# A hybrid encoder on one core: attention starts from half blocks kept in SBUF, and four smaller moves in the DeltaNet stage

## The chip, the cores and the metric

The kernel runs on 1 core of a Trainium2 chip. The metric is the device time of one execution in microseconds; three runs of the kernel before gave a median of 2773.81 us (2767.05 to 2774.55).

## The reference, cut to what matters

One encoder layer on two sequences, x_sample (2048 tokens) and x_prompt (1024 tokens), 1024 channels each, in float32. One projection feeds two branches, which are merged by gates.

```python
def _encoder_layer(x, ...):
    h = _rms_norm(x, norm_g)
    proj = jnp.einsum('btd,de->bte', h, w_in)
    qkv_a, z_a, qkv_b, z_b, beta_raw, alpha_raw, gate_a, gate_b = jnp.split(proj, split_points, axis=-1)
    ...
    o_a = _neighbourhood_attention(q_a, k_a, qkv_a[:, :, 2], rpb).reshape(B, T, NA_WIDTH) * jax.nn.silu(z_a)
    y_a = jnp.einsum('bte,ed->btd', o_a, w_branch_a)
    o_b = _deltanet_branch(qkv_b, z_b, beta_raw, alpha_raw, conv_w, a_log, dt_bias, dn_norm_g)
    y_b = jnp.einsum('bte,ed->btd', o_b, w_branch_b)
    merged = jax.nn.sigmoid(gate_a) * y_a + jax.nn.sigmoid(gate_b) * y_b
    return x + jnp.einsum('btd,de->bte', merged, w_out)
```

The DeltaNet branch convolves q, k and v along the tokens, and then runs one chunked delta-rule scan in each direction, for which it solves triangular systems (here: "inverses"). The attention branch has 8 heads of 64 and looks at a window of 8 rows by 16 columns on a grid 64 wide.

## The kernel before

The 3072 tokens are 6 blocks of 512, each in two half blocks of 256 columns; blocks 0 to 3 are the sample, 4 and 5 the prompt. The work comes in three stages.

**DeltaNet** (`deltanet()`). The normalised input is split into a high and a low float16 part, `hh` and `hl`, tiles of 128 x 8 x 256 in the pool `hp` with two buffers each; a copy of every half block is kept in DRAM (`hdr`). The projections' 36 tiles of 128 output channels (`Tile`, kinds r, z and g) go over the half blocks in five passes of twelve, n = 0 to 59: the first twelve come from the input, and the others are read back from `hdr` by four DMAs that `launch()` issues once half block n - 2 is used up. A tile on a half block is 24 products (`pp`) with the scaled weights `w`; ACT evacuates it (`evacuate`), kind g by a tanh into `thz` and a store to DRAM (`gtd`) for the last stage. The weights of later tiles come in by two generators `weights(0)` and `weights(1)`, half a tile each: a pass of maxima (`amax` on `wst`, tile `wm`), `factors()`, which reduces the maxima (`wma`), spreads them over the partitions by transposes on TensorE (`pm`) and makes scales of them, and then the split into float16 parts.

The order is a table of slots. `step_slot()` issues, on engines whose order is pinned to program order, what was put off to this slot, then a step of the scans (S), of the inverses (I), of weights (W) and rows (H), and of operands (O), with products from `products()` (`fill()`) poured between them up to a quarter, a half, three quarters and the whole of a slot's budget; `mids` and `ends_`, calls put there by `mid()` and `end()`, come at three quarters; then the finishing steps (F). A generator's `yield` ends its part of a slot, `yield 2` waits two slots. Where `fill()` has no product to give, it issues dummy transposes (`idle`) up to half the budget. `inverse()` reads the diagonal blocks of its matrices back from DRAM (`ed`) into `X` and `YT`, two slots later copies a part of `YT` transposed into `X` on ACT and on DVE, and works on from there; its sums run on DVE, and results go back through DRAM (`rd`, `RR`). `finish()` normalises a finished block: squares on ACT, a power on POOL (`af`), a scaling on ACT (`P<-P,af`), four transposes on TensorE (`ptf`), another scaling on ACT and a store (`obd`). At the stage's end `weights(1)` puts the first head pair's attention weights in DRAM (`wt`, `wt0` in the code), and `out_blocks()` prepares the output weights (`wod`).

**Attention**. For each of four head pairs, each block is projected by `proj_mm`, 4 tiles of tokens with 24 products each (`ppn`), with half blocks `H[b]` (`rh`, `rl`) as the stationary side and the pair's weights (`whi`, `wlo`) as the moving one. The blocks come in the order 4, 5, 0, 1, 2, 3. After the second block the first units (scores, exp, values) begin. `H` stays in SBUF through the stage: blocks 4 and 5 in the pool `h1`, the others in `hr`. In the fourth head pair, `branch_weights` puts the branch weights (`y`) in the places of blocks 4 and 5.

**Output**. The branch products are merged with the gates, and the last product is done.

At the boundary, deltanet's pools are closed, those of attention opened in the same SBUF, and 50 dummy transposes issued while the first weights and block 4 come in, pinned no longer: DMAs are ordered by a scheduler there.

Of the kernel before, what the change touches and what calls it, by code (L numbers as in the profile page):

```python
# [8 lines left out]
F32 = mybir.dt.float32  # L9
# [14 lines left out]
BLK = 512  # L24
# [21 lines left out]
def emit(nc, tc, x_prompt, x_sample, norm_g, w_in, attn_q_norm_g, attn_k_norm_g, attn_rpb, dn_conv_w, dn_a_log,  # L46
# [120 lines left out]
    def deltanet():  # L167
# [13 lines left out]
        ps_mm = opn("ps_mm", bufs=2, space=PSUM)  # L181
        hp = opn("hp", bufs=2, side="right")
        TR = (ps_tr, "tr", 4)


        sn = 0
        later, mids, ends_ = {}, [], []
        gens = {c: [] for c in "SOIFHW"}

# [26 lines left out]
        def fill(u):  # L216

            while T.cost < u:
                if not next(filler, 0):

                    t = ps_tr.tile([128, 4, 128], F32, name="idle", tag="tr") if T.cost < WARM * u else None
                    while T.cost < WARM * u:
                        T.transpose(t[:, 0, :], ident, ident)
                    return
# [39 lines left out]
        for n, t in enumerate(tiles):  # L264
            t.n = n
        wsc, wfc = (dcp.tile([128, NT + 5], F32, name=n) for n in ("wsc", "wfc"))
# [18 lines left out]
        def small():  # L285

            cwr = wk.tile([60, 128], F32, name="cwr", tag="gr", bufs=1)
# [12 lines left out]
            V.tensor_scalar_mul(nal, nal, -1.0)  # L300
# [136 lines left out]
        def staged(src, k):  # L437

            n = src.shape[0] // 256
            st = wk.tile([128, n, src.shape[1]], F32, name="wst", tag="xt", bufs=2)  # L440
            end(SY.dma_start, st, src[128 * n * k:128 * n * k + 128 * n].rearrange("(k p) c -> p k c", p=128))
            return st
# [41 lines left out]

        sb = wk.tile([128, 8, 16], F32, name="sb", tag="raw1")
        fba_ = []
# [8 lines left out]
        def bias_table():  # L495
# [6 lines left out]
            rp = wk.tile([120, 64], F32, name="rp", tag="gr", bufs=1)  # L502
            rp, ng = rp[:, 0:31], rp[:, 32:64]
# [13 lines left out]
            for ct in range(3):  # L517
                SY.dma_start(ud[16 * ct:16 * ct + 16].rearrange("i r k -> r i k"), ng[:, None, :].to_broadcast([120, 16, 32]))
            yield 3
            for ct, off in enumerate((0, -8, -16)):  # L520
# [9 lines left out]
        def weights(k):  # L530
# [9 lines left out]
            for p in range(1, 5):  # L540
# [3 lines left out]
                if k:  # L544
                    while maxed[0] < maxed[1]:
                        yield
                    yield from factors(ts[0].n, ts[-1].n + 1, ts)
                    facs[0] = p
                    yield
# [16 lines left out]
            while maxed[0] < maxed[1]:  # L566
                yield

            m1 = sm.tile([128, 2], F32, name="am1", bufs=1)
# [30 lines left out]
        def out_blocks(k):  # L600
# [4 lines left out]
            for i in range(k, 16, 2):  # L605
                p, q = divmod(i, 4)
                st = wk.tile([128, 4, 128], F32, name="wst", tag="raw1", bufs=2)
# [4 lines left out]
                hi, lo = (wk.tile([128, 7, 128], F16, name="wos", tag=t, bufs=2) for t in ("raw0", "raw2"))  # L612
                S.activation(hi[:, 0:3], st[:, 1:4], AF.Identity, scale=so4)
# [50 lines left out]
        def evacuate(t, n, pp):  # L664
            b, j = divmod(n, 2)
            f = wfc[:, t.n:t.n + 1]
            if t.kind == "r":
                if j == 0:
                    raws[t.h, b, t.i] = wk.tile([128, BLK + 4], F32, name=f"raw{t.i}")
# [7 lines left out]
            if t.kind == "g":  # L677
                SY.dma_start(gtd[n][t.i], th)
                return
# [78 lines left out]
        def tables(u):  # L758
# [48 lines left out]
            T.transpose(pr[:64, :], gc.rearrange("p a b -> p (a b)"), ident)  # L807
            gr = wk.tile([64, 128], F32, name="gr", tag="gr", bufs=1)
            V.tensor_copy(gr, pr[:64, :])
# [177 lines left out]
        def inverse(h, it):  # L987
# [4 lines left out]

            X = wk.tile([128, 1056], F32, name="X", bufs=1)
            U = wk.tile([128, 1024], F32, name="YT", bufs=1)
            W = wk.tile([128, 704], F32, name="Yo", bufs=1)
            Xr, Ur = (t[:, 0:1024].rearrange("p (r k) -> p r k", r=32) for t in (X, U))
# [4 lines left out]
            yield 2  # L1001
            S.activation(Xr[32:64], Ur[32:64].rearrange("p r k -> p k r"), AF.Copy)
            V.tensor_copy(Xr[96:128], Ur[96:128].rearrange("p r k -> p k r"))
            yield
# [58 lines left out]
            yield 1  # L1063
            RR = wk.tile([128, 2, 512], F32, name="RR", tag="X", bufs=1)
            Rc, Rt = (RR[:, q].rearrange("p (d c k) -> p d c k", d=2, c=8) for q in range(2))
# [73 lines left out]

            ZZ = wk.tile([128, 384], F32, name="ZZ", tag="YT", bufs=1)  # L1140
            Z = ZZ[:, 0:128].rearrange("p (c k) -> p c k", c=4)
# [77 lines left out]
        def finish(o):  # L1219
# [18 lines left out]
            for c in range(4):  # L1238
                T.transpose(pt[:, c, :], M[:, c, :], ident)
            ot = M.rearrange("p c t -> p (c t)")  # L1240
            S.activation(ot, pt.rearrange("p c t -> p (c t)"), AF.Identity, scale=dngz[:, o.h:o.h + 1])
# [11 lines left out]
        def launch():  # L1253
            l = todo["half"]
            if l and rel.get(l[0] - 2, sn) < sn:
                n = l.pop(0)
                t = half_tiles()
                for i in range(2):
                    for j in range(2):
                        f = SY.dma_start, t[i][:, 4 * j:4 * j + 4], hdr[n % 12 // 2][:, i, n % 2, 4 * j:4 * j + 4]  # L1260
                        if i + j:
                            at(i + j, *f)
                        else:
                            f[0](*f[1:])
                at(4, halves.__setitem__, n, t)
# [92 lines left out]
        while stk:  # L1358
            close(stk.pop())

    deltanet()

# [118 lines left out]
    def proj_mm(w, b, t):  # L1481

        hh, hl = H[b]
        ts = slice(128 * t, 128 * t + 128)
        pp = ps_mm.tile([128, 384], F32, name="ppn", tag="mm")
# [172 lines left out]
    def branch_weights(n):  # L1658

        for e in range(8):  # L1660
            if e % 2 == 0:
                y = h1.tile([128, 2, 2, 2, 4, 128], F16, name=f"y{e}", tag="h", bufs=4)
                for i in range(2):
                    for j in range(2):
                        wy[e + i, j] = y[:, i, j, 0], y[:, i, j, 1]
# [5 lines left out]
    for b in (4, 5, 0, 1, 2, 3):  # L1671
        H[b] = [(h1 if b > 3 else hr).tile([128, 8, BLK], F16, name=f"r{n}{b}", tag="h", bufs=4 if b > 3 else 8)
                for n in "hl"]
# [7 lines left out]

    t = ps_mm.tile([128, 256], F32, name="idle", tag="mm")
    for _ in range(50):
        T.transpose(t[:, 0:128], ident, ident)

    for k in (slice(0, 4), slice(4, 8)):
        for i, t in enumerate((w.hi, w.lo)):
            SY.dma_start(t[:, :, k], wt0[:, 3072 * i:3072 * i + 3072].rearrange("p (j k c) -> p j k c", j=3, k=8)[:, :, k])
            SY.dma_start(H[4][i][:, k, 0:HB], hdr[4][:, i, 0, k])
    for i in range(2):  # L1690
        SY.dma_start(H[4][i][:, :, HB:BLK], hdr[4][:, i, 1])
    w.p = [abp[:, 4 + j:5 + j] for j in range(3)]
    pair_scales(w, V)
    load_H(5)

# [248 lines left out]
    for hp_ in range(4):  # L1944
        if hp_:
            w = nxt
        if hp_ < 3:
            nxt = pair(hp_ + 1)
            next_pair(nxt)
        for b, ats in ((4, ()), (5, (5, 4)), (0, ()), (1, (0,)), (2, (1,)), (3, (2, 3))):  # L1950
            if hp_ == 3 and b == 0:
# [7 lines left out]
            if hp_ == 0 and b in (4, 5, 0, 1):  # L1959
                with tc.issue_after(anchors[b].ins):  # L1960
                    load_H((2, 3, None, None, 0, 1)[b])
            for a in ats:
# [67 lines left out]
    while stk:  # L2030
        close(stk.pop())
    close(p_cp)
    close(p_dr)
# [22 lines left out]
```

## Time and profile before

| | |
|---|---|
| runs, median | 2773.81 us |
| profiled execution | 2774.7 us, span 2772.9 us |
| TensorE busy | 2693.2 us, 97% |
| mean granted TensorE clock | 0.993 |
| dummy transposes | 274, 36.4 us |
| last product of DeltaNet ends about | 1654.4 us |
| first product of attention | 1668.0 us |

In the rows of a timeline stand the start, the length, the engine, the instruction with what it writes and reads, how often in a row, and in brackets how long the engine had been idle and what ended that. An instruction's length overlaps with its neighbours' on TensorE, so counts of them are best costed by the length of a row with many. Nearly every instruction has line 61, a helper that pins the order, so groups go by tiles.

### The profile page before, as it was taken

The page shows a single profiled execution, that of the slowest core. Times are in us where ns is not written, and L with a number is a line of the kernel's source. Part 1 is how long each engine was busy: PE and PEld are TensorE (multiplying, and loading weights), DVE is VectorE, ACT ScalarE, POOL GpSimd, SP SyncE. Part 2 cuts the span into 40 slices and gives each one's busy share as a digit, 9 for nine tenths or more (in the row PEclk, how much of TensorE's full clock was granted, in tenths as well). Part 3 has the DMA queues.
Part 4 walks back from the last instruction along what each step waited for, and adds up shares of the span by engine and source line. Part 5 has one row for each costly group of instructions (what it writes and reads, how often), then busy time and mean ns, then how long its engine had stood idle before and what let it go on. Part 6 is the DMA issues. An engine that isn't in the chain of part 4 may idle for free.

```text
span 2772.9 us, 65318 instructions
## 1 busy us (share of the span) xinstructions
PE 2693.2 (97%) x25080; PEld 2160.1 (78%) x25080; DVE 1763.7 (64%) x4099; ACT 1392.1 (50%) x3861; POOL 962.9 (35%) x1737
## 2 busy tenths in 40 slices
PE   7999999999999999999999999999999999999999
PEld 6888888988889888999888896666666666776675
DVE  6767866576775766747666423666666677556654
ACT  4455564555545655455554534666666764211211
POOL 2233231231222322222322305445444444554453
PEclk9999999999999999999999999999999999999999
DMA  7433442354533444323446648433332565444341
GB/s 244 156 118 92 126 128 85 106 150 112 131 101 104 131 135 127 89 89 108 123 118 179 187 126 222 120 112 89 102 94 86 151 205 200 167 168 158 115 146 69
DMA packets 503974, 365.02 MB, mean 132 GB/s; under 512 B 146035, under 2 KB 452847, under 8 KB 502767
## 3 DMA queue, kind: packets, MB, share of 16 engines
q1 hardware_dynamic: 503663, 360.85, 43.7%
q8 instruction: 198, 3.24, 0.5%
q14 instruction: 113, 0.93, 0.1%
HBM read 262.53 MB, written 98.20 MB: 130 GB/s over the span
## 4 chain that ended last, share of the span: by engine, by line
PE 73%; DVE 11%; DMA 5%; ACT 4%; SPq 3%; issue 2%; POOL 1%; DVEq 0%; POOLq 0%; ACTq 0%
PE pp L61 31%; PE ppn L61 10%; PE pk L61 6%; SPq L61 3%; DVE YT L61 2%; PE pT L61 2%; PE pS L61 2%; PE lv L61 2%; PE pon L61 1%; DVE P L61 1%; DVE Yo L61 1%; PE gq L61 1%; ACT P L61 1%; PE ptk L61 1%; PE idle L61 1%
## 5 line engine op out<-in xcount | busy, mean ns | idle before, releaser
L61 PE MATMUL pp<-hh,w 128*128 128x256 f16 x6912 | 1197.1, 274 | 13.7 <-DVE thz L61 8.4
L61 PEld LDWEIGHTS <-w 128*128 128x128 f16 x10368 | 1013.8, 99 | 146.0 <-issue 13.3
L61 PE MATMUL pp<-hl,w 128*128 128x256 f16 x3456 | 948.4, 274 | 6.1 <-DMA hl<-hdr 3.8
L61 PE MATMUL ppn<-whi,rh 128*128 128x384 f16 x768 | 250.4, 326 | 1.6 <-ACT qs L61 1.6
L61 PEld LDWEIGHTS <-y 128*128 128x128 f16 x2304 | 224.7, 98 | 34.7 <-issue 6.6
L61 PE MATMUL ppn<-whi,rl 128*128 128x384 f16 x768 | 251.3, 327 | 0.0
L61 PE MATMUL ppn<-wlo,rh 128*128 128x384 f16 x768 | 250.4, 326 | 0.0
L61 PEld LDWEIGHTS <-rh 128*128 128x128 f16 x1536 | 144.6, 98 | 71.7 <-issue 1.8
L61 POOL TENSOR_TENSOR th<-th 128x128 f32<-128x128 f32 (+1 forms) x240 | 148.2, 635 | 145.7 <-DVE th L61 132.5
L61 PEld LDWEIGHTS <-mm 128*128 128x128 f16 x1008 | 98.6, 98 | 115.2
L61 ACT ACTIVATE thz<-pp,wfc 128x256 f32<-128x256 f32 x288 | 124.0, 472 | 122.5 <-PE pp L61 92.7
L61 ACT ACTIVATE mm<-th 128x256 f16<-128x256 f32 x144 | 58.9, 445 | 227.9 <-POOL th L61 227.9
L61 DVE TENSOR_TENSOR pl<-pT,ph 128x384 f16<-128x384 f32 (+1 forms) x192 | 110.8, 599 | 82.1 <-ACT ph L61 80.8
L61 POOL TENSOR_TENSOR rqk<-rqk,mhalf 128x4 f32<-128x4 f32 x48 | 51.9, 1081 | 293.7 <-DVE rqk L61 287.3
L61 DVE CUSTOM_DVE_ANT_0 Sb<-pS,bt 128x384 f32<-128x384 f32 (+1 forms) x192 | 108.8, 598 | 67.0 <-DMA vd<-vt 23.5
L61 ACT ACTIVATE vn<-pk,nbeg 128x128 f32<-128x128 f32 x176 | 65.1, 370 | 160.6 <-PE pk L61 160.2
L61 ACT ACTIVATE Sb<-Sb,nm,pq 128x384 f32<-128x384 f32 (+1 forms) x192 | 140.0, 733 | 1.2 <-DVE nm L61 1.1
L61 PEld LDWEIGHTS <-rl 128*128 128x128 f16 x768 | 74.9, 98 | 61.2 <-issue 30.1
L61 ACT ACTIVATE raw<-pp,wfc 128x256 f32<-128x256 f32 x144 | 63.7, 472 | 116.7 <-PE pp L61 113.7
L61 ACT ACTIVATE Os<-pon,rsn 128x64 f32<-128x64 f32 x192 | 49.9, 312 | 142.8 <-PE pon L61 142.7
L61 DVE SCALAR_TENSOR_TENSOR P<-raw,cw,P 128x512 f32<-128x512 f32 x144 | 116.1, 806 | 0.6
L61 DVE SCALAR_TENSOR_TENSOR S<-S,egl,pk 128x128 f32<-128x128 f32 x160 | 54.8, 343 | 91.2 <-PE pk L61 67.1
(621 smaller groups left out, 5653.4 us busy)
## 6 DMA issues: line engine op xcount, KB each, us to landing
wst<-in_w_in SPq DMA_DIRECT2D x124, 256.0 KB
gtd<-thz SPq DMA_DIRECT2D x192, 128.0 KB
hh<-hdr SPq DMA_DIRECT2D x96, 256.0 KB
hl<-hdr SPq DMA_DIRECT2D x96, 256.0 KB
th<-gtd SPq DMA_DIRECT2D x24, 1024.0 KB
vw<-vd SPq DMA_DIRECT2D x320, 64.0 KB
IT<-gd SPq DMA_DIRECT2D x48, 256.0 KB
bt<-ud SPq DMA_DIRECT2D x256, 48.0 KB
```

The costliest lines, as they stand in the source:

```text
L61: i = f(*a, **k)
```

## The change

Seven edits:

- The pool `hp` is opened ahead of `deltanet()` and stays open; the last two half blocks (n = 58 and 59, block 5) are kept as `kept`. Attention does block 5 first, from them, and block 4 second; block 4 alone is loaded at once, and block 5's copies in `h1` are gone. Half of the branch weights go to the two places of `hp`.
- The 50 dummies are gone, and `fill()` issues none once all 24 blocks have had their last transposes (`finished`).
- Tiles whose last use is early (X, YT, Yo, raw, staged weights and some small ones) go to a pool `we` on the right side of SBUF, where attention later has its first weights.
- The stores of the last four gate tiles on the last three half blocks (twelve DMAs) are issued from ACT's queue.
- The first two copies of each inverse are put to the slot's end (`end`).
- The generators of weights wait one slot more between the last maximum and `factors()`, and between the last maximum and the last scales.
- The three stores of the bias table's blanks come two slots apart.

```diff
+        we = opn("we", bufs=2, side="right")
...
             while T.cost < u:
                 if not next(filler, 0):
+                    if finished[0] == 4 * NB:
+                        return
...
-            t.n = n
+            t.n, t.last = n, n > len(tiles) - 5
...
-            yield 3
+                yield 2
+            yield
...
                     while maxed[0] < maxed[1]:
                         yield
+                    yield
                     yield from factors(ts[0].n, ts[-1].n + 1, ts)
...
-                SY.dma_start(gtd[n][t.i], th)
+                (S if t.last and n > 8 else SY).dma_start(gtd[n][t.i], th)
...
-            X = wk.tile([128, 1056], F32, name="X", bufs=1)
+            X = we.tile([128, 1056], F32, name="X", bufs=1)
...
             yield 2
-            S.activation(Xr[32:64], Ur[32:64].rearrange("p r k -> p k r"), AF.Copy)
-            V.tensor_copy(Xr[96:128], Ur[96:128].rearrange("p r k -> p k r"))
+            end(S.activation, Xr[32:64], Ur[32:64].rearrange("p r k -> p k r"), AF.Copy)
+            end(V.tensor_copy, Xr[96:128], Ur[96:128].rearrange("p r k -> p k r"))
             yield
...
                 T.transpose(pt[:, c, :], M[:, c, :], ident)
+            finished[0] += 1
...
+                if n >= 58:
+                    kept[n - 58] = t
...
+    p_hp, hp = pool("hp", bufs=2, side="right")
+    kept = {}
     deltanet()
...
-        hh, hl = H[b]
-        ts = slice(128 * t, 128 * t + 128)
+        hh, hl = H[b] if b < 5 else kept[t // 2]
+        ts = slice(128 * (t if b < 5 else t % 2), 128 * (t if b < 5 else t % 2) + 128)
...
-                y = h1.tile([128, 2, 2, 2, 4, 128], F16, name=f"y{e}", tag="h", bufs=4)
+                if e < 4:
+                    y = h1.tile([128, 2, 2, 2, 4, 128], F16, name=f"y{e}", tag="h", bufs=2)
+                    y = y[:, 0], y[:, 1]
+                else:
+                    y = [hp.tile([128, 2, 2, 4, 128], F16, name=f"y{n}{e}", tag=n) for n in ("hh", "hl")]
...
-    t = ps_mm.tile([128, 256], F32, name="idle", tag="mm")
-    for _ in range(50):
-        T.transpose(t[:, 0:128], ident, ident)
-
     for k in (slice(0, 4), slice(4, 8)):
         for i, t in enumerate((w.hi, w.lo)):
             SY.dma_start(t[:, :, k], wt0[:, 3072 * i:3072 * i + 3072].rearrange("p (j k c) -> p j k c", j=3, k=8)[:, :, k])
-            SY.dma_start(H[4][i][:, k, 0:HB], hdr[4][:, i, 0, k])
-    for i in range(2):
-        SY.dma_start(H[4][i][:, :, HB:BLK], hdr[4][:, i, 1])
...
-    load_H(5)
+    load_H(4)
...
-        for b, ats in ((4, ()), (5, (5, 4)), (0, ()), (1, (0,)), (2, (1,)), (3, (2, 3))):
+        for b, ats in ((5, ()), (4, (5, 4)), (0, ()), (1, (0,)), (2, (1,)), (3, (2, 3))):
```

On TensorE at the boundary, this stands in the program before (`pp` is DeltaNet's product, `ptf` the last two blocks' transposes, `ppn` attention's first products; LDWEIGHTS is the load of the stationary side):

```order
22910 L61 MATMUL pp<-hl,w 128x256
22911 L61 LDWEIGHTS w
22912 L61 MATMUL pp<-hh,w 128x256
22913 L61 MATMUL idle<-ident 128x128 x30
22914 L61 MATMUL ptf<-ident,P 128x128 x8
22915 L61 MATMUL idle<-ident 128x128 x84
22916 L61 LDWEIGHTS rh_23722
22917 L61 MATMUL ppn<-whi,rh_23722 128x384
```

In the change the only dummies near the end stand ahead of the last half block's products, and then the first projection follows, on the kept half block:

```order
22716 L61 MATMUL pp<-hl,w 128x256
22717 L61 LDWEIGHTS w
22718 L61 MATMUL pp<-hh,w 128x256
22719 L61 MATMUL idle<-ident 128x128 x17
22720 L61 LDWEIGHTS w
22721 L61 MATMUL pp<-hh,w 128x256
```

```order
22910 L61 MATMUL pp<-hl,w 128x256
22911 L61 LDWEIGHTS w
22912 L61 MATMUL pp<-hh,w 128x256
22913 L61 LDWEIGHTS hh
22914 L61 MATMUL ppn<-whi,hh 128x384
```

114 dummies have become 17, the eight `ptf` now stand at 22840, ahead of the last 36 products, and the stationary side of `ppn` is `hh` instead of `rh`.

On DVE at the fifth inverse (`X<-YT` is its first copy, `thz<-thz,pp` the evacuation that frees a bank for TensorE, `P` and `Vt` with `raw` are steps of the convolution, `w` is a weight's low part), before:

```order
801 L61 SCALAR_TENSOR_TENSOR t<-pk,egc,Vt 128x128
802 L61 COPY X<-YT 32x1024
803 L61 SCALAR_TENSOR_TENSOR w<-wst,wsc,w 128x512 x2
804 L61 SCALAR_TENSOR_TENSOR P<-raw_8328,cw,P 128x512
805 L61 SCALAR_TENSOR_TENSOR Vt<-raw_8652,cw,Vt 128x512
806 L61 SCALAR_TENSOR_TENSOR thz<-thz,pp 128x256
```

and in the change:

```order
801 L61 SCALAR_TENSOR_TENSOR t<-pk,egc,Vt 128x128
802 L61 SCALAR_TENSOR_TENSOR P<-raw_8333,cw,P 128x512
803 L61 SCALAR_TENSOR_TENSOR Vt<-raw_8657,cw,Vt 128x512
804 L61 COPY X<-YT 32x1024
805 L61 SCALAR_TENSOR_TENSOR thz<-thz,pp 128x256
806 L61 MEMSET X 128x32
807 L61 SCALAR_TENSOR_TENSOR w<-wst,wsc,w 128x512 x2
```

Two steps of the convolution have moved ahead of the copy, the weight's low part behind it, and `thz` stands right behind the copy. At the first inverse the step `P<-raw_1836,P`, which `ptk` on TensorE reads, has moved from behind the copy to ahead of it in the same way.

On SP at the boundary (`gtd<-thz` are the gate stores, `obd<-P` finished blocks, `rh` and `rl` block 4), before:

```order
682 L61 DMA gtd_100<-thz 128x256 x4
683 L61 DMA whi<-wt_102 128x3x512
684 L61 DMA rh_23722<-hdr_69 128x4x256
685 L61 DMA obd_76<-P 128x512
686 L61 DMA obd_75<-P 128x512
687 L61 DMA wlo<-wt_102 128x3x512
688 L61 DMA rl_23723<-hdr_69 128x4x256
```

and in the change, where the weights are issued:

```order
662 L61 DMA wt_102<-w 128x1024 x2
663 L61 DMA obd_72<-P 128x512
664 L61 DMA whi<-wt_102 128x3x512
665 L61 DMA wlo<-wt_102 128x3x512
666 L61 DMA whi<-wt_102 128x3x512
667 L61 DMA gtd_96<-thz 128x256 x2
668 L61 DMA wlo<-wt_102 128x3x512
669 L61 DMA hh<-hdr_69 128x1024
```

The weights' loads have moved from behind the last gate stores to right behind the stores of `wt`, ahead of the loads of half block 57 (`hh<-hdr_69`) and of the last two; block 4's copies stand at 684, behind `obd_75`, `otn` and three loads of `bt`.

More of the change, by code (lines that the diff above doesn't have):

```diff
@@ L181, in deltanet @@
         ps_mm = opn("ps_mm", bufs=2, space=PSUM)
-        hp = opn("hp", bufs=2, side="right")
+        we = opn("we", bufs=2, side="right")
         TR = (ps_tr, "tr", 4)
@@ L187, in deltanet @@
         later, mids, ends_ = {}, [], []
+        finished = [0]
         gens = {c: [] for c in "SOIFHW"}
@@ L285, in small @@
         def small():
-            cwr = wk.tile([60, 128], F32, name="cwr", tag="gr", bufs=1)
+            cwr = we.tile([60, 128], F32, name="cwr", tag="gr", bufs=1)
             SY.dma_start(cwr, dn_conv_w[0].rearrange("t (g p) -> (t g) p", p=128))
@@ L439, in staged @@
             n = src.shape[0] // 256
-            st = wk.tile([128, n, src.shape[1]], F32, name="wst", tag="xt", bufs=2)
+            st = we.tile([128, n, src.shape[1]], F32, name="wst", tag="xt", bufs=2)
             end(SY.dma_start, st, src[128 * n * k:128 * n * k + 128 * n].rearrange("(k p) c -> p k c", p=128))
@@ L483, in first_weights @@
                 yield
-        sb = wk.tile([128, 8, 16], F32, name="sb", tag="raw1")
+        sb = we.tile([128, 8, 16], F32, name="sb", tag="raw1")
         fba_ = []
@@ L501, in bias_table @@
                 SY.dma_start(gk2[64 * j:64 * j + 64], attn_k_norm_g[0].rearrange("(p o) -> p o", o=1))
-            rp = wk.tile([120, 64], F32, name="rp", tag="gr", bufs=1)
+            rp = we.tile([120, 64], F32, name="rp", tag="gr", bufs=1)
             rp, ng = rp[:, 0:31], rp[:, 32:64]
@@ L567, in weights @@
                 yield
+            yield
             m1 = sm.tile([128, 2], F32, name="am1", bufs=1)
@@ L606, in out_blocks @@
                 p, q = divmod(i, 4)
-                st = wk.tile([128, 4, 128], F32, name="wst", tag="raw1", bufs=2)
+                st = we.tile([128, 4, 128], F32, name="wst", tag="raw1", bufs=2)
                 for j, (a, b) in enumerate(((0, 1), (0, 0), (1, 0), (1, 1))):
@@ L611, in out_blocks @@
                 yield 2
-                hi, lo = (wk.tile([128, 7, 128], F16, name="wos", tag=t, bufs=2) for t in ("raw0", "raw2"))
+                hi, lo = (we.tile([128, 7, 128], F16, name="wos", tag=t, bufs=2) for t in ("raw0", "raw2"))
                 S.activation(hi[:, 0:3], st[:, 1:4], AF.Identity, scale=so4)
@@ L668, in evacuate @@
                 if j == 0:
-                    raws[t.h, b, t.i] = wk.tile([128, BLK + 4], F32, name=f"raw{t.i}")
+                    raws[t.h, b, t.i] = we.tile([128, BLK + 4], F32, name=f"raw{t.i}")
                 S.activation(raws[t.h, b, t.i][:, 2 + HB * j:2 + HB * j + HB], pp, AF.Identity, scale=f)
@@ L807, in tables @@
             T.transpose(pr[:64, :], gc.rearrange("p a b -> p (a b)"), ident)
-            gr = wk.tile([64, 128], F32, name="gr", tag="gr", bufs=1)
+            gr = we.tile([64, 128], F32, name="gr", tag="gr", bufs=1)
             V.tensor_copy(gr, pr[:64, :])
@@ L991, in inverse @@
             rd = dr.tile([2, 8, 4, 32, 32], F32, name=f"rd{h}{it}")
-            X = wk.tile([128, 1056], F32, name="X", bufs=1)
-            U = wk.tile([128, 1024], F32, name="YT", bufs=1)
-            W = wk.tile([128, 704], F32, name="Yo", bufs=1)
+            X = we.tile([128, 1056], F32, name="X", bufs=1)
+            U = we.tile([128, 1024], F32, name="YT", bufs=1)
+            W = we.tile([128, 704], F32, name="Yo", bufs=1)
             Xr, Ur = (t[:, 0:1024].rearrange("p (r k) -> p r k", r=32) for t in (X, U))
@@ L1063, in inverse @@
             yield 1
-            RR = wk.tile([128, 2, 512], F32, name="RR", tag="X", bufs=1)
+            RR = we.tile([128, 2, 512], F32, name="RR", tag="X", bufs=1)
             Rc, Rt = (RR[:, q].rearrange("p (d c k) -> p d c k", d=2, c=8) for q in range(2))
@@ L1138, in level4 @@
                     V.tensor_copy(u.E[u.A:u.A + 64, :, u.B:u.B + 64], lv[u.A:u.A + 64])
-            ZZ = wk.tile([128, 384], F32, name="ZZ", tag="YT", bufs=1)
+            ZZ = we.tile([128, 384], F32, name="ZZ", tag="YT", bufs=1)
             Z = ZZ[:, 0:128].rearrange("p (c k) -> p c k", c=4)
@@ L1661, in branch_weights @@
             if e % 2 == 0:
-                y = h1.tile([128, 2, 2, 2, 4, 128], F16, name=f"y{e}", tag="h", bufs=4)
+                if e < 4:
[3 more added lines that the diff above has]
+                    y = [hp.tile([128, 2, 2, 4, 128], F16, name=f"y{n}{e}", tag=n) for n in ("hh", "hl")]
                 for i in range(2):
                     for j in range(2):
-                        wy[e + i, j] = y[:, i, j, 0], y[:, i, j, 1]
+                        wy[e + i, j] = y[0][:, i, j], y[1][:, i, j]
             for j in range(2):
@@ L1670, in emit @@
     H = [None] * NB
-    for b in (4, 5, 0, 1, 2, 3):
-        H[b] = [(h1 if b > 3 else hr).tile([128, 8, BLK], F16, name=f"r{n}{b}", tag="h", bufs=4 if b > 3 else 8)
+    for b in (4, 0, 1, 2, 3):
+        H[b] = [(h1 if b > 3 else hr).tile([128, 8, BLK], F16, name=f"r{n}{b}", tag="h", bufs=2 if b > 3 else 8)
                 for n in "hl"]
@@ L1960, in emit @@
                 with tc.issue_after(anchors[b].ins):
-                    load_H((2, 3, None, None, 0, 1)[b])
+                    load_H((2, 3, None, None, 1, 0)[b])
             for a in ats:
@@ L2031, in emit @@
         close(stk.pop())
+    close(p_hp)
     close(p_cp)
```

## The prediction

> **What bounds the kernel now.** I read the page first, then PE's waits, then PE's timeline around each wait, then the other engines there, and last the granted clock by windows.
>
> ```profile
> span 2772.9 us, 65318 instructions
> PE 2693.2 (97%) x25080; PEld 2160.1 (78%) x25080; DVE 1763.7 (64%) x4099; ACT 1392.1 (50%) x3861; POOL 962.9 (35%) x1737
> 1600.00:1620.00 20.00, 20.00 (x184) 18.61 (x182) 5.78 (x20) 7.05 (x21) 0.00 (x0) 1.00 0.37 119
> ```
>
> The span is TensorE's: it is busy for 2693.2 of 2772.9 us, and in a stretch near the end of DeltaNet for 20.00 of 20.00 (third row: window, its length, then each engine's busy time, TensorE first, the granted clock, the DMA share and GB/s). The change takes no product away, so it can save three things: TensorE's idle time (79.7 us in all), dummy transposes that count as busy, and time at a lower clock. The waits of TensorE (engine, tile, what it waited for, us in total, times, longest) show where the idle time lies:
>
> ```profile
> PE pp L61 <- DVE thz L61: 8.6, 5, 3.1
> PE ptk L61 <- DVE P L61: 5.0, 4, 3.2
> PE pm L61 <- DVE wma L61: 3.7, 3, 2.6
> PE pp L61 <- DMA hl<-hdr: 3.8, 2, 3.3
> ```
>
> Each of these totals is mostly one or two single waits, so each can be looked up. The timeline of the boundary, where DeltaNet ends and attention begins (start, length, instruction, count):
>
> ```profile
> 1640.76 0.61 PE L61 MATMUL pk<-vn,IT 128*128 128x128 f32 x4
> 1654.42 3.44 PE L61 MATMUL idle<-ident 128*128 128x128 f32 x30
> 1657.69 1.04 PE L61 MATMUL ptf<-ident,P 128*128 128x128 f32 x8
> 1658.57 9.60 PE L61 MATMUL idle<-ident 128*128 128x128 f32 x84
> 1668.00 0.33 PE L61 MATMUL ppn<-whi,rh 128*128 128x384 f16 x1
> 1655.40 2.44 ACT L61 ACTIVATE P<-P,af 128x128 f32<-128x128 f32 x8
> 1657.61 0.37 SPq L61 DMA_DIRECT2D whi<-wt  x1
> 1663.57 1.00 SPq L61 DMA_DIRECT2D rl<-hdr  x1
> ```
>
> TensorE does 114 dummy transposes between the last projection of DeltaNet and the first of attention, because the weights (whi) and block 4 (rh, rl) are issued only from 1657.61 on. The page calls this busy.
>
> **Part by part: the boundary.** The 114 dummies cost 3.44 + 9.60 = 13.04 us, 0.114 us each. The order of the change has 17 there, 1.95 us, and the first projection follows at once on the last DeltaNet product: -11.1 us. Elsewhere it has 163 dummies for 160: +0.3. What covers the rest:
>
> ```profile
> 1643.99 10.59 PE pp L61 x97
> 1668.17 14.14 PE ppn L61 x86
> 1674.41 2.00 SPq L61 DMA_DIRECT2D rl<-hdr  x1
> 1670.43 0.10 PEld L61 LDWEIGHTS <-rl 128*128 128x128 f16 x1 [0.38 <-DMA rl<-hdr]
> ```
>
> A DeltaNet product takes 10.59/97 = 0.109 us, an attention one 14.14/86 = 0.164. The last transposes (ptf) need a chain through DVE, ACT, POOL and ACT again that took 16.3 us here (pk's end at 1641.4 to 1657.69); in the change 156 products and the 17 dummies stand in between, 19.0 us, so ptf should not wait. Weights: issued two half blocks early. Block 4 is now the second block, wanted 4 x 24 x 0.164 = 15.7 us after the first projection. Its copy stands on SP behind two stores of P that follow ptf, a load of otn and three of bt. Estimate: ptf ends 36 x 0.109 = 3.9 us before the first projection, the stores land at most 5.9 us after their issue (rl took 1670.43 - 1664.57 = 5.9 from issue to use, with much in flight), and I give ACT's copies and SP's issues 3 us, so block 4 is issued from 5.0 us on; at 2.0 us a DMA (1674.41) its first half is issued by 9.0 and lands by 14.9 of 15.7. The nearest other case, block 5 in this trace, was issued to 1676.4 and wanted at 1668.2 + 15.7 = 1683.9 without a wait. I take zero, and 0 to 5 us as the bounds. Swapping blocks 4 and 5, and putting the later branch weights where the kept halves were, adds no instruction: zero, covered by the three blocks between the last read of the halves and their overwriting.
>
> **The inverses' first copies.** They are ACT and DVE instructions that wait for a DMA, and everything queued behind them waits too:
>
> ```profile
> L61 ACT ACTIVATE X<-YT 32x1024 f32<-32x1024 f32 x12 | 23.9, 1996 | 13.9 <-DMA YT<-ed 13.7
> 205.84 1.06 DVE L61 COPY X<-YT 32x1024 f32<-32x1024 f32 x1 [3.80 <-DMA YT<-ed]
> 209.92 0.63 PE L61 MATMUL ptk<-ident,P 128*128 128x128 f32 x4 [3.16 <-DVE P L61]
> 664.27 1.07 DVE L61 COPY X<-YT 32x1024 f32<-32x1024 f32 x1 [4.54 <-DMA YT<-ed]
> 668.03 0.41 DVE L61 SCALAR_TENSOR_TENSOR thz<-thz,pp 128x256 f32<-128x256 f32 x1
> 668.49 0.37 PE L61 MATMUL pp<-hh,w 128*128 128x256 f16 x1 [3.14 <-DVE thz L61]
> 1023.09 1.06 DVE L61 COPY X<-YT 32x1024 f32<-32x1024 f32 x1 [3.81 <-DMA YT<-ed]
> 1027.31 0.27 PE L61 MATMUL pp<-hh,w 128*128 128x256 f16 x1 [2.40 <-DVE thz L61]
> ```
>
> Three of twelve inverses reach TensorE: 3.16, 3.14 and 2.40 us. In the change the product for ptk (P) stands ahead of the copy, so the first goes. In the other two, thz stands right behind the copy instead of five instructions behind it: at 668 it would end at 664.27 + 1.07 + 0.41 = 665.8 instead of 668.4, which leaves some 0.5 us of the wait (TensorE had arrived at 668.49 - 3.14 = 665.35); at 1027 it goes. That is 3.16 + 2.7 + 2.4 = 8.3 us. The copy itself is 2.0 us on ACT and delays the same slot's end; X's next user, a memset a slot later, has the time.
>
> **The extra yield before the scale factors.**
>
> ```profile
> 1331.30 0.69 DVE L61 TENSOR_REDUCE wm<-wst 128x1 f32<-128x512 f32 x1 [2.99 <-DMA wst<-in_w_in]
> 1332.87 0.16 DVE L61 TENSOR_REDUCE wma<-wm 128x4 f32<-128x8 f32 x1
> 1333.17 0.76 PE L61 MATMUL pm<-ident,wma 128*128 128x128 f32 x4 [2.65 <-DVE wma L61]
> ```
>
> TensorE stood 2.65 us at transposes whose input DVE was late with. A slot later the input is long there: -2.65. The weights come a slot later for it; the dummies, which count the starved slots, hardly change (+3), so I cost that at zero.
>
> **The clock.** After such waits the granted clock (third number from the end) is down:
>
> ```profile
> 668.00:672.00 4.00, 3.51 (x20) 2.87 (x20) 2.46 (x9) 3.46 (x8) 2.53 (x3) 0.58 0.62 197
> 672.00:676.00 4.00, 4.00 (x39) 3.63 (x38) 3.79 (x11) 0.69 (x2) 0.96 (x1) 1.00 0.00 0
> 200.00:220.00 20.00, 16.84 (x213) 14.80 (x211) 13.15 (x26) 8.56 (x23) 8.47 (x14) 0.91 0.54 186
> 660.00:680.00 20.00, 16.86 (x142) 14.82 (x141) 13.82 (x33) 11.73 (x31) 6.76 (x10) 0.91 0.36 101
> 1320.00:1340.00 20.00, 17.35 (x258) 13.87 (x257) 13.60 (x28) 10.78 (x34) 9.29 (x18) 0.91 0.66 194
> 1020.00:1040.00 20.00, 17.60 (x161) 15.85 (x160) 15.46 (x35) 13.00 (x37) 6.24 (x10) 1.00 0.46 123
> ```
>
> 20 x 0.09 = 1.8 us are lost behind each of three of the waits, none behind the one at 1027: another -5.4 if these waits go. The Trainium skill's page "TensorE: Matmul & The Clock Gate", Part 1, has the clock fall to half rate after an idle window of about 3.4 us, and speaks for dummies wherever a wait could be that long. By it none of these waits (3.16, 3.14, 2.65 us) would have cost clock, this term would be nothing and the time 2757.9. The rows show the half rate (0.58 over 4 us) but already behind 2.65 us, so they decide: -5.4.
>
> **Stores and the rest.** Twelve gate stores (gtd) move to ACT's queue, where each takes issue time:
>
> ```profile
> 1631.04 0.79 SPq L61 DMA_DIRECT2D gtd<-thz  x2
> L61 ACT ACTIVATE thz<-pp,wfc 128x256 f32<-128x256 f32 x288 | 124.0, 472 | 122.5 <-PE pp L61 92.7 <-issue 28.3 <-ACT Yo L61 0.5
> ```
>
> 0.4 us each, and ACT has per pair of evacuations 48 x 0.109 = 5.2 us for 2 x 0.47 + 2 x 0.4 + at most 2.44 (P<-P,af) = 4.2: hidden. The bias table's pauses move SP work that no TensorE wait follows: zero. The weights' four loads go ahead of a half block's on SP; bound 0 to 5 us, taken as zero, since TensorE lacked nothing in that stretch (1600 to 1620, above).
>
> **Sum.** -11.1 + 0.3 - 8.3 - 2.65 - 5.4 = -27.1 us. Other order also makes other waits; I allow one new wait like the largest that stays:
>
> ```profile
> 617.28 0.37 PE L61 MATMUL pp<-hl,w 128*128 128x256 f16 x1 [3.30 <-DMA hl<-hdr]
> 617.00:621.00 4.00, 3.72 (x39) 2.59 (x42) 3.96 (x8) 0.00 (x0) 1.51 (x4) 0.61 1.00 309
> ```
>
> 3.30 + 4 x 0.39 = 4.9 us. So -22.2. The profiled execution took 2774.7 us with its span of 2772.9, 0.9 us above the median of the runs (2773.81); 2774.7 - 22.2 = **2752.5 us**, span near 2750.7. A measurement of this kernel can tell about 0.3%, 8.3 us, from no change.
>
> **Rivals.**
> - Waits only move: the DMAs land no sooner, and other work then stands behind the copies. For it: the copies' DMA waits stay on the queues. Against it: the named products are ahead of them. Only the boundary counts: 2774.7 - 10.8 = 2764.
> - Block 4 or the early weights come late: 5 us and a clock loss of 1.7 at one place, 2752.5 + 6.7 = 2759. For it: 14.9 of 15.7 us above.
> - Slower: ACT, in order, must wait at each store until an earlier transfer has landed, and thz behind it does not free its bank. Six pairs, two stores each; free time per pair is 1.0 us, 3.4 where no P work falls. With 5.9 us a store, 2 x 5.9 - 3.4 = 8.4 us a pair, six pairs 50 us: 2803. The gain is eaten from 2w - 3.4 = 22.2/6, w = 3.6 us. Against it: SP issues its gate stores at 0.4 us each, two in a row, without standing between them.
> - No change: the weights land no earlier, since their place in SBUF frees late, and TensorE stands for 11 us where it did dummies; with the inverses' waits moved too, 2774. Against it: the loads are ahead of the last half blocks on SP, and these cannot run without theirs.
>
> **Numbers.** Forecast 0.66, waits only move 0.19, late copies 0.07, slower 0.04, no change 0.04. The first three are faster by over 8.3 us except for a tail of 0.04 of them: faster 0.88, same 0.08, slower 0.04. Range: above, the boundary alone with half a new wait, 2764 + 2.5 = 2766.5, about 2767; below, the whole 27.1 and the wait at 617 gone too, 2774.7 - 32.0 = 2742.7, cut to 2744, since nothing in the change acts on that wait directly.
>
> **What would show it.** Right: 17 dummies and no TensorE wait between the last pp and the first ppn; no waits over 1 us behind X<-YT; pm without its 2.65; clock 1.00 in these windows; about 79.7 - 8.3 - 2.65 = 69 us idle in all, and some 3 more for the new wait. Wrong: a wait in the last three half blocks of DeltaNet with ACT standing at a store, a wait for rh or rl some 16 us after the first ppn, or as much idle time as before with other names.

## The result, and the profile after

The change is slower: 2788.51 us in the median of four runs (2786.14 to 2791.3) against 2774.18, a ratio of 1.006 (95% interval 1.0045 to 1.0074). I had forecast 2752.5 us, 2744 to 2767. (In e2, e3, e5 and e13 below, one execution each took 3417 to 9207 us, and the ratios leave it out.) The page of the change, its span and the engines' busy time:

```profile
span 2787.8 us, 65131 instructions
PE 2688.4 (96%) x24986; PEld 2152.3 (77%) x24986; DVE 1762.4 (63%) x4099; ACT 1396.3 (50%) x3861; POOL 963.3 (35%) x1737
```

TensorE issues 94 instructions fewer (25080 before), which are the dummies; at 0.114 us they are 10.7 us. It is idle for 2787.8 - 2688.4 = 99.4 us instead of 79.7, 19.7 more. Summed over windows of 20 us (length times the missing share), the granted clock loses 29.6 us instead of 21.2, 8.4 more. The three make +17.4, near the 14.9 by which the span grew. So the dummies went, and new waits took more than they gave.

The boundary came out as forecast but for one wait. Its timeline, TensorE, then ACT:

```profile
1663.90 2.02 PE L61 MATMUL idle<-ident 128*128 128x128 f32 x17
1672.31 1.04 PE L61 MATMUL ptf<-ident,P 128*128 128x128 f32 x8
1678.72 0.34 PE L61 MATMUL ppn<-whi,hh 128*128 128x384 f16 x1 [1.45 <-ACT thz L61]
1677.82 0.33 ACTq L61 DMA_DIRECT2D gtd<-thz  x1
1678.19 0.47 ACT L61 ACTIVATE thz<-pp,wfc 128x256 f32<-128x256 f32 x1 [0.40 <-ACT thz L61]
```

Seventeen dummies instead of 114, no wait for weights or for block 4; the only wait is 1.45 us for the last gate's evacuation, whose neighbour's store stands in front of it on ACT. The loss lies earlier. The finishing transposes ptf mark the same step in both kernels. Before, then the change:

```profile
484.89 1.04 PE L61 MATMUL ptf<-ident,P 128*128 128x128 f32 x8
1200.93 1.04 PE L61 MATMUL ptf<-ident,P 128*128 128x128 f32 x8
```

```profile
475.48 1.04 PE L61 MATMUL ptf<-ident,P 128*128 128x128 f32 x8
1212.59 1.04 PE L61 MATMUL ptf<-ident,P 128*128 128x128 f32 x8
```

The change is 9.4 us ahead at the first (about 3.6 of them are clock at the start, see the last section) and 11.7 behind at the second: 21 us are lost between them, where the scans, inverses and weights run side by side. The place of the old wait of 3.14 us (668.49 before) shows what happened; ACT, then DVE, then TensorE:

```profile
655.13 1.50 ACT L61 ACTIVATE w<-wst,wsc 128x512 f16<-128x512 f32 x2 [4.75 <-DMA wst<-in_w_in]
656.65 1.94 ACT L61 ACTIVATE X<-YT 32x1024 f32<-32x1024 f32 x1
650.49 1.06 DVE L61 COPY X<-YT 32x1024 f32<-32x1024 f32 x1
659.55 0.80 PE L61 MATMUL pk<-vn,kh 128*128 128x128 f32 x2 [4.03 <-ACT P L61]
```

The copies no longer wait for their own transfer here (over all twelve, ACT's waits for it fall from 13.7 us to 3.8). But ahead of ACT's copy now stands a split of weights (w) that waits 4.75 us for its load (wst), and behind both stands the scan's P, for which TensorE stands 4.03 us. Later, the chain from SP through DVE to TensorE:

```profile
1065.10 2.57 SPq L61 DMA_DIRECT2D rd<-Yo  x4
1069.98 5.60 SPq L61 DMA_DIRECT2D ed<-P  x8
1075.62 0.98 SPq L61 DMA_DIRECT2D IT<-gd  x2
1076.70 1.01 SPq L61 DMA_DIRECT2D wst<-in_w_in  x2
1083.27 1.47 DVE L61 TENSOR_REDUCE wm<-wst 128x1 f32<-128x512 f32 x2 [6.14 <-DMA wst<-in_w_in]
1086.35 0.33 DVE L61 SCALAR_TENSOR_TENSOR S<-S,egl,pk 128x128 f32<-128x128 f32 x1
1086.74 1.22 PE L61 MATMUL pk<-S,KQ 128*128 128x128 f32 x4 [3.15 <-DVE S L61]
```

SP issues the weights' load at 1076.70, behind the inverse's stores rd and eight stores ed; DVE asked for it at 1083.27 - 6.14 = 1077.1 and stands, since the two loads need until 1083.27; the scan's S stands behind the maximum, and TensorE waits 3.15 us. SP's own waits from 1050 to 1090 us show what held it up: gate stores for thz, loads of wst for the splits (w) that still read their buffer, the read-back for rd, the stores ed for P.

```profile
SPq L61 <- DVE w L61: 6.9, 5, 3.5
SPq L61 <- ACT thz L61: 5.7, 1, 5.7
SPq L61 <- DVE P L61: 1.9, 1, 1.9
SPq L61 <- DMA rd<-Yo: 1.7, 1, 1.7
```

The largest new wait comes the same way, with the evacuation thz behind the maxima; DVE, then TensorE:

```profile
973.85 1.52 DVE L61 TENSOR_REDUCE wm<-wst 128x1 f32<-128x512 f32 x2 [5.99 <-DMA wst<-in_w_in]
977.07 0.37 PE L61 MATMUL pp<-hh,w 128*128 128x256 f16 x1 [4.79 <-DVE thz L61]
```

Six times in the change ACT or DVE stands 4.2 to 6.8 us for a load of wst, and TensorE 2.7 to 4.8 us behind it (at 660, 768, 977, 1087, 1545 and 1564 us): 20.2 us in all. The clock goes with these waits; at 1080 us (window, length, busy times, then the granted clock, third from the end):

```profile
1080.00:1090.00 10.00, 6.85 (x98) 5.38 (x97) 5.13 (x11) 4.71 (x13) 4.05 (x5) 0.79 0.70 206
```

### The profile page after: what moved, and what is told of

Its sections match the earlier page's. It is cut to its first block, busy times and chain, and to the rows that moved or that the text cites. A ratio compares the mean times of both kernels' runs of the same rounds, so it can differ in the third digit from the quotient of the medians.

```text
span 2787.8 us, 65131 instructions
## 1 busy us (share of the span) xinstructions
PE 2688.4 (96%) x24986; PEld 2152.3 (77%) x24986; DVE 1762.4 (63%) x4099; ACT 1396.3 (50%) x3861; POOL 963.3 (35%) x1737
## 4 chain that ended last, share of the span: by engine, by line
PE 51%; DVE 5%; DMA 2%; SPq 2%; ACT 1%; issue 1%; POOL 1%; DVEq 0%; ACTq 0%; POOLq 0%
PE pp L61 13%; PE ppn L61 10%; PE pk L61 3%; PE pT L61 2%; SPq L61 2%; PE pS L61 2%; PE pon L61 2%; DVE YT L61 1%; PE lv L61 1%; DVE P L61 1%; PE pqk L61 1%; PE pO L61 0%; DVE Yo L61 0%; DVE Sb L61 0%; DMA wst<-in_w_in 0%
## 5 line engine op out<-in xcount | busy, mean ns | idle before, releaser
L61 PE MATMUL ppn<-whi,rh 128*128 128x384 f16 x640 | 209.0, 327 | 2.2 <-ACT qs L61 2.2
L61 PE MATMUL ppn<-whi,rl 128*128 128x384 f16 x640 | 209.8, 328 | 0.0
L61 PE MATMUL ppn<-wlo,rh 128*128 128x384 f16 x640 | 209.0, 327 | 0.0
L61 PEld LDWEIGHTS <-rh 128*128 128x128 f16 x1280 | 120.5, 98 | 60.2 <-issue 2.6
L61 PEld LDWEIGHTS <-y 128*128 128x128 f16 x1152 | 112.3, 98 | 20.3 <-issue 5.1
L61 PE MATMUL pk<-S,KQ 128*128 128x128 f32 x704 | 101.1, 278 | 9.7 <-DVE S L61 9.3
```

What stands on the lines that cost most here:

```text
L61: i = f(*a, **k)
```

## Theories and experiments

Theory W: the two extra yields in `weights(1)` shift the weights by a slot against the inverses, and the waits above follow. Theory C: the copies at the slot's end stand in front of the next scan step. Theory P: the bias table's pauses put its stores among the weights' loads. Within W: W-SP blames the loads' place on SP, W-wait the standing for loads, W-work the place of the weights' own DVE and ACT work. Ratios are to the kernel before on the same chip, medians beside them.

**e1, no yields.** The change without:

```diff
-                    yield
                     yield from factors(ts[0].n, ts[-1].n + 1, ts)
...
-            yield
 
             m1 = sm.tile([128, 2], F32, name="am1", bufs=1)
```

> The change without its two extra yields in weights(1); all else as changed. Theory W (weights): the yields shift the weights by a slot against the inverses, so that the loads of wst stand on SP behind the inverses' stores (rd, ed) and DVE and ACT stand at wm, w and wos for them, with the scans behind; most of the 28 us that DeltaNet loses between 698 and 1235 us comes from this: 2760 to 2766 us. Theory C (copies at the slot's end stand in front of the next slot's scan step): about as the change, 2788 us. Theory P (the pauses in the bias table): about 2788 us.

Measured: 2755.93 us, 0.9936 (0.9915 to 0.9958), 4 us under what Theory W gave. W holds; C and P are out as the main cause. The place of the chain above, in e1:

```profile
1059.33 1.27 DVE L61 TENSOR_REDUCE wm<-wst 128x1 f32<-128x512 f32 x2
1065.28 1.00 SPq L61 DMA_DIRECT2D wst<-in_w_in  x2
```

```profile
1060.00:1090.00 30.00, 30.00 (x446) 25.38 (x444) 17.03 (x33) 19.00 (x58) 14.35 (x25) 1.00 0.45 129
```

The maxima there find their loads without a wait, and TensorE is busy for 30.00 of 30.00 us at full clock. None of the six pairs of waits is left there; the longest pair of this kind in DeltaNet is the old one, 2.95 us of DVE and 2.61 of TensorE at 1322. In all, e1's trace has 24.6 us less idle time of TensorE than the change's (74.8 against 99.4) and 13.8 us less lost clock (15.8 against 29.6).

**e2, copies as before.**

```diff
-            end(S.activation, Xr[32:64], Ur[32:64].rearrange("p r k -> p k r"), AF.Copy)
-            end(V.tensor_copy, Xr[96:128], Ur[96:128].rearrange("p r k -> p k r"))
+            S.activation(Xr[32:64], Ur[32:64].rearrange("p r k -> p k r"), AF.Copy)
+            V.tensor_copy(Xr[96:128], Ur[96:128].rearrange("p r k -> p k r"))
```

> The change with the inverses' first copies where they were before. Theory W: the copies' waits come back, 2788 to 2797 us. Theory C: 2760 to 2768 us. Theory P: 2788 us or a little more.

Measured: 2777.12 us, 1.0015 (1.0003 to 1.0028). Neither: beside the yields the moved copies cost about 11 us (2788.5 against 2777.1) instead of saving as many, which no theory had.

**e3, pauses as before.**

```diff
-                yield 2
-            yield
+            yield 3
             for ct, off in enumerate((0, -8, -16)):
```

> The change with the bias table's pauses as before (three slots after the three stores instead of two after each and one more). Theory P: the stores of the table come four slots later, among the loads of wst, and cost the time; without them 2762 to 2770 us. Theories W and C: 2785 to 2790 us.

Measured: 1.0059 (1.0039 to 1.0079), the change's 1.006 again. Theory P is out.

**e4, the boundary alone:** the three edits above together.

> The boundary alone: kept half blocks, early weights, block 5 ahead of block 4, the branch weights' new places, the pool on the right and the gate stores on ACT, but copies, yields and pauses as before. All three theories: faster than before by the 97 dummies (11 us) less up to 4 us that attention's end lost in the change: 2763 to 2768 us. If it is no faster than before, the loss in DeltaNet comes from the boundary's own edits, which none of the three says.

Measured: 2767.49 us, 0.9978 (0.9963 to 0.9993), in the range; the gain is 6 us. Its order has 30 dummies at the boundary where the change has 17; it issues 24996 instructions on TensorE, 84 fewer than before, which are 9.6 us.

**e9, the weights' loads on ACT.**

```diff
-            end(SY.dma_start, st, src[128 * n * k:128 * n * k + 128 * n].rearrange("(k p) c -> p k c", p=128))
+            end(S.dma_start, st, src[128 * n * k:128 * n * k + 128 * n].rearrange("(k p) c -> p k c", p=128))
```

> The whole change, with the weights' loads (wst in staged) issued by ACT instead of SP; TensorE's order is the same. Theory W-SP: after the yields these loads stand on SP behind the inverses' stores and reads, land 6 us after DVE and ACT ask for them, and that is the loss; on another queue they land in time, the waits for wst go, and the time falls to 2758 to 2768 us. Rival theory W-work: the loads are not to blame, the weights' own DVE and ACT work (1.4 us pieces) now lies in front of the scans in full slots: 2785 us or more, ACT's issue time coming on top.

Measured: 2778.2 us, 1.0015 (1.0004 to 1.0026): between the two, and no verdict by itself; e10 below is its base.

**e8, two slots.** `yield 2` at both places instead of `yield`.

> The change with pauses of two slots instead of one at both places. Theory W-SP says that it matters which of the inverses' slots the loads meet: a second slot moves them on, so the time can be anywhere from 2756 to 2790 us and need not be above the change's 2788; the dummies stay near 180. Rival (lateness: the weights come too late for the products): worse than one slot, 2800 us or more, with more dummies or with waits of pp for w.

Measured: 2784.09 us, 1.0035 (1.0018 to 1.0052). Not worse than one slot, and TensorE issues 24988 instructions against 24986, so hardly a dummy more: lateness is out.

**e7, only the yield ahead of m1.** The change without the first line of e1's diff.

> The change without the yield ahead of the factors, but with the one ahead of m1. By the alignment of the traces 28 of the 36 us between the change and the kernel without both yields are lost ahead of 1400 us, where only the factors' yield acts: 2760 to 2766 us. Rival: the m1 yield, which shifts the last weights and the output weights wos, holds most of the loss: 2780 us or more.

Measured: 2755.42 us, 0.9932 (0.9906 to 0.9958), as e1. Within the noise the whole loss is the yield ahead of the factors; I had expected up to 8 us from the other.

**e5, the yields alone,** added to the kernel before.

> The kernel before with the two yields alone. Theory W-SP: the loads meet the inverses' stores here too; without the copies' move the runs so far give 10 us for it (2777 against 2767): 2780 to 2786 us. Rival (the yields hurt only together with the moved copies, which pull the inverses' later steps into the same slots): 2770 to 2775 us, as before. My prediction's own term (2.65 us and a clock loss saved) would give 2768 to 2770.

Measured: 2786.06 us, 1.0044 (1.0029 to 1.006). They cost 12 us alone and 34 us in the change (1.0060 against 0.9936). With the boundary's edits but without the copies' move they and the pauses cost 10 us (e2 against e4, 1.0015 against 0.9978): they hurt without the copies' move, and some three times as much with it.

**e11, no waits for the loads.** In the change (and, as e12, in e1) the maxima and splits of the later weights read `ident`, the matrix of the transposes, instead of the loaded weights; the loads are still issued, but no instruction waits for them, and no load waits for a reader of its buffer:

```diff
-            amax(wm2[:, n, k:k + 1], st)
+            V.tensor_reduce(wm2[:, n, k:k + 1], ident[:, None, :].to_broadcast([128, 4, 128]), axis=AX.XY, op=MAX, apply_absolute_value=True)
...
-            S.activation(t.w_[:, 0, ks], st, AF.Identity, scale=s)
+            res = ident[:, None, :].to_broadcast([128, 4, 128])
+            S.activation(t.w_[:, 0, ks], res, AF.Identity, scale=s)
...
-            V.scalar_tensor_tensor(t.w_[:, 1, ks], in0=st, scalar=s, in1=t.w_[:, 0, ks], op0=MUL, op1=SUB)
+            V.scalar_tensor_tensor(t.w_[:, 1, ks], in0=res, scalar=s, in1=t.w_[:, 0, ks], op0=MUL, op1=SUB)
```

> The whole change, but the weights' maxima and splits of the four later tiles of every stream read a constant that lies in SBUF; the loads of wst are still issued, and nobody reads them, so no maximum or split waits for a load and no load waits for a maximum or split. The projections so use wrong weights. To be compared with the kernel that does the same without the yields (e12_resident_no_yield). Theory W-wait: what the yields cost is DVE and ACT standing for late loads, with the scans behind them: the two differ by at most 8 us instead of the 32 between the change and e1_no_yields, and this one takes 2745 to 2765 us. Theory W-work: the weights' work itself lies badly one slot later: they still differ by 25 us or more, and this one takes 2780 us or more.

> The same reading of a constant in e1_no_yields (wrong weights here too). Both theories: 2745 to 2756 us, a little under e1_no_yields; it is the base for e11_resident.

Measured: 2762.89 us, 0.9958 (0.9944 to 0.9971), and 2753.61 us, 0.9932 (0.9912 to 0.9952). The pages of e11 and of e12:

```profile
span 2760.7 us, 65045 instructions
PE 2678.4 (97%) x24986; PEld 2146.7 (78%) x24986; DVE 1762.7 (64%) x4099; ACT 1397.0 (51%) x3861; POOL 972.0 (35%) x1737
```

```profile
span 2751.3 us, 65030 instructions
PE 2675.7 (97%) x24996; PEld 2146.6 (78%) x24996; DVE 1766.7 (64%) x4099; ACT 1395.0 (51%) x3861; POOL 971.8 (35%) x1737
```

The yields still cost 7 us by the ratios and 9 by the medians, where they cost 32 to 34 with the waits; TensorE is idle for 82.3 and 75.6 us. Theory W-wait holds for about three quarters of the loss, if it is taken to mean all waits between the loads and their readers, SP's for a free buffer too: the edit takes both away at once. The rest, hardly above the noise, is W-work's, or that of loads that are still read (wos, the attention weights).

**e10, e1 with the loads on ACT** (e9's edit).

> e1_no_yields with the weights' loads on ACT's queue. If loads that stand on SP still cost where there are no yields, 2748 to 2753 us; if the few waits that are left there come from elsewhere, 2755 us or, with ACT's issue time on the path, 2760.

Measured: 2776.6 us, 1.0005 (0.9987 to 1.0023), some 20 us slower than e1, which neither expectation had. TensorE's waits there, the largest two but for the start:

```profile
PE lv L61 <- ACT Q L61: 12.0, 10, 2.7
PE pk L61 <- ACT P L61: 6.0, 3, 2.4
```

ACT is late with the inverses' Q (4.0 us of waits in e1) and the scans' P, its own queue standing at loads now: ahead of thz and P it stands 10.6 and 10.1 us until DVE's splits are done with a load's buffer, and never for these in e1. Against this base the yields cost about 3 us (1.0015 against 1.0005), no difference clear of noise. Whether the loads' phase matters less off SP, or the 20 us of other waits hide it, is not shown.

**e13, boundary and copies only** (the change without yields and pauses).

> The boundary's edits and the copies at the slot's end, without yields and without the bias table's pauses. The copies alone should make the difference to e4_boundary (2767): my prediction's terms for them (8.3 us of waits, 3.6 of clock) give 2755 to 2759 us, the same as e1_no_yields, if the pauses cost and save nothing; if the pauses matter, it is 5 us or more away from e1_no_yields' 2756.

Measured: 0.9932 (0.9911 to 0.9953), as e1: the pauses cost and save nothing. Against e4 (0.9978), which differs by the copies alone, it is 13 us faster: without the yields the copies' move pays here too.

**e14, loads ahead in the slot,** and e15, the same in e1.

```diff
-            end(SY.dma_start, st, src[128 * n * k:128 * n * k + 128 * n].rearrange("(k p) c -> p k c", p=128))
+            SY.dma_start(st, src[128 * n * k:128 * n * k + 128 * n].rearrange("(k p) c -> p k c", p=128))
```

> The whole change, but the weights' loads (staged) are issued by SP at the weights' step itself instead of at the slot's three quarters: on SP they so stand ahead of the same slot's stores of ed, gates and the like, still behind the stores of rd; TensorE, DVE and ACT keep their order but for buffer names. Theory W-SP (the place on SP makes the loads late): a large part of the 32 us comes back, 2760 to 2772 us. Rival (the transfers are slow from traffic, whatever their place on SP): 2783 us or more.

> The same earlier issue without the yields. Theory W-SP: little is left to gain there, 2750 to 2757 us, so that the yields cost at most 15 us where the loads stand ahead. Rival: 2756 us, and the yields still cost 27 us or more.

Measured: 2780.64 us, 1.0022 (1.0006 to 1.0039), and 2759.78 us, 0.9943 (0.9925 to 0.9961). The earlier place (the weights' step at half the slot instead of three quarters) saves 8 to 11 us in the change and nothing in e1, so the yields cost 22 us instead of 32 to 34: more than W-SP said, less than its rival. The trace tells why; SP, then DVE, of e14:

```profile
1057.80 2.58 SPq L61 DMA_DIRECT2D rd<-Yo  x4
1062.53 5.40 SPq L61 DMA_DIRECT2D ed<-P  x8
1067.97 0.98 SPq L61 DMA_DIRECT2D IT<-gd  x2
1069.05 1.00 SPq L61 DMA_DIRECT2D wst<-in_w_in  x2
1075.72 0.69 DVE L61 TENSOR_REDUCE wm<-wst 128x1 f32<-128x512 f32 x1 [5.89 <-DMA wst<-in_w_in]
```

The load that costs most still stands behind the stores rd and ed of the step before, and DVE stands 5.89 us for it. A quarter of a slot was not enough there.

**e6, the copies alone,** e2's diff the other way round in the kernel before.

> The kernel before with only the inverses' first copies moved to the slot's end. By my prediction's terms 8.3 us of waits and 3.6 us of clock go: 2760 to 2766 us. Rival (waits only move): 2771 to 2776 us.

Measured: 2764.05 us, 0.9961 (0.9946 to 0.9975): 11 us, the prediction's term. Its trace has no wait of over 0.9 us for P or thz near 209 and 668, and at 1027 one of 1.58 is left of 2.40:

```profile
1022.54 0.27 PE L61 MATMUL pp<-hh,w 128*128 128x256 f16 x1 [1.58 <-DVE thz L61]
```

But this trace, of the slowest of the eight executions (2771.81 us), is idle for 78.3 us, only 1.4 less than before: other waits have grown (hl at 615 us 4.05 instead of 3.30, pqk 2.94 instead of 1.82). The mean granted clock of the eight is 0.995 against 0.993 for the kernel before, an estimated 6 of the 11 us.

The fastest kernels with the right weights are e1, e7 and e13, at 0.993: the change without the yield ahead of the factors is faster than both kernels.

## Why the prediction was wrong

**The step that failed** is the sentence "The weights come a slot later for it; the dummies, which count the starved slots, hardly change (+3), so I cost that at zero." I asked whether TensorE would lack weights, and it did not (e8). I did not ask what else is a slot later: every load that the generator issues on SP, and every maximum and split that waits for it in order on DVE and ACT with the scans behind. The prediction's own row at 1331.30 shows a maximum that stands 2.99 us for its load, ahead of the wait that the yield was to remove. That wait went, as said: 0.6 us in all for wma, instead of 3.7. The yield was to save 2.65 us of it and 1.8 of clock; the yields cost 12 us alone (e5), 34 in the change (e1). Shown is that it is this yield (e7), that some three quarters of it is waits between the loads and their readers (e11 against e12), and that a quarter of a slot on SP is worth a third of it (e14 against e15). How much of these waits is SP's place and how much the loads' own way, some 6 us from issue to landing at 1077, was not taken apart further. That SP cannot pass a store that waits is seen in its own waits at 1050 to 1090, 5.7 us of them for one gate store; the Trainium skill's page "DMA: Bandwidth & Descriptors" says it in "Anatomy of one DMA — SWDGE (gpsimd) path": a wait for a semaphore is made on the issuing sequencer, before dispatch. The trace agrees for SP, by these 5.7 us.

**The copies** were right in size: 8.3 us of waits and 3.6 of clock were forecast, 11 us measured alone (e6), 13 beside the boundary (e13 against e4). In mechanism they were right for the three named waits, of which 8.70 us became at most 0.84 + 1.58 in e6's trace; that the rest of that trace gives most of it back was not foreseen. Beside the yields the same move costs 11 us (e2), and why it turns is open; the rows at 655 show one way, a copy that now stands behind a waiting split.

**The boundary** was right up to the first projection, but for the 1.45 us: 17 dummies, no wait for weights or block 4. It was wrong behind it: I took attention as unchanged, and e4 gains 6 us where its 84 dummies are 9.6. In e4 attention begins earlier and meets its first units' loads; DVE's waits there:

```profile
1723.40 0.56 DVE L61 CUSTOM_DVE_ANT_0 Sb<-pS,bt 128x384 f32<-128x384 f32 x1 [3.67 <-DMA bt<-ud]
1727.40 0.56 DVE L61 CUSTOM_DVE_ANT_0 Sb<-pS,bt 128x384 f32<-128x384 f32 x1 [3.44 <-DMA vw<-vd]
```

TensorE waits 3.92 us behind them, 1.82 before. Around 2200 to 2300 us stand waits of 1 to 2 us in both kernels, 8.9 us in e4 and 5.4 before. No run took this apart.

**Gate stores on ACT:** right by the trace. An issue takes 0.33 us, and the next evacuation starts 0.40 us after the one before it ended; at none of the twelve stores did ACT stand for an earlier transfer, so the slower rival, which I gave 0.04, was the wrong mechanism on the right side. **The pauses:** zero, as said (e3, e13).

**The clock:** I gave three waits 1.8 us each. The same pm wait stands before at 1333.17 and in e1 at 1322.05; first the window of before, then e1's row and its window:

```profile
1320.00:1340.00 20.00, 17.35 (x258) 13.87 (x257) 13.60 (x28) 10.78 (x34) 9.29 (x18) 0.91 0.66 194
```

```profile
1322.05 0.62 PE L61 MATMUL pm<-ident,wma 128*128 128x128 f32 x4 [2.61 <-DVE wma L61]
```

```profile
1320.00:1340.00 20.00, 17.50 (x245) 14.93 (x246) 12.42 (x27) 9.80 (x32) 6.14 (x11) 1.00 0.41 127
```

2.65 us cost clock there, 2.61 here did not. In the change the wait for wma is gone and the clock is not back: 0.96 and 0.95 over the two windows from 1320 to 1360, 1.8 us, around a wait of 1.90 us. A wait of this size may or may not cost clock, so the term was what one execution happened to show, written as a sure sum.

**The rivals.** "Waits only move" named the mechanism, and I priced it at no gain; that moved waits can be more and longer than the old ones was in no rival and not in the allowance of 4.9 us for one new wait. The range so ended 7 us under the old time. The last sign of being wrong, "as much idle time as before with other names", is what came: 99.4 us where 69 to 72 were forecast.

## What to carry to other kernels

A pause in one stream of a static, in-order schedule moves all that the stream issues: list its DMAs and the instructions that wait for them, and look in each new slot at what they stand behind on the queue and what stands behind them on the engines. An edit that saves one wait of 2.65 us by shifting a whole stream should be tried apart from the edits that it comes with. Move the waiting instruction, as the copies' edit does, rather than its stream.

## What the runs showed of the hardware that was not expected

The clock at the start differs between profiles with the same waits. Before, then the change:

```profile
20.00:80.00 60.00, 56.46 (x606) 48.85 (x605) 43.66 (x79) 29.12 (x57) 14.22 (x39) 0.91 0.73 234
```

```profile
20.00:80.00 60.00, 56.44 (x651) 50.69 (x650) 47.34 (x90) 32.90 (x66) 14.86 (x42) 1.00 0.79 254
```

The same stretch has TensorE busy for 56.46 and 56.44 us, with the same two waits in it (1.27 and 0.93 us before, 1.28 and 0.93 after), and is granted 0.91 and 1.00: 60 x 0.09 = 5.4 us between two profiles that no wait of TensorE in it explains. From 80 to 100 us it is the other way round, 1.00 before and 0.91 in the change, so that 3.6 us stay. There the same wait for thz stands in both (2.67 us at 96.14 before, 2.65 at 91.56 in the change), and the 4 us behind it are granted 1.00 before and 0.57 in the change. In windows of 20 us the losses are mostly 0.09 or 0.17, one or two times 1.8 us. The Trainium skill's page "TensorE: Matmul & The Clock Gate", Part 1, has the activity window run freely, not from the kernel's start, so that the same code meets it in another phase from run to run; the two profiles agree with that.
